# Activation sums by product, squares added by DMA, weight sums in place, and a down stage that begins with four units

## The chip, the cores and the metric

The kernel runs on one core of a Trainium2 chip. The metric is device time in microseconds for one execution of the whole program. A core has TensorE (matrix multiplication), VectorE, ScalarE, POOL (GpSimd) and SyncE, each with its own instruction order, and DMA queues that SyncE, ScalarE and POOL issue to.

## The reference

One decoder layer on 512 tokens of width 2048, in float32: a mixer of three head groups, a cross-attention into 256 memory tokens, and a gated MLP, each behind an RMSNorm and with a residual add; a last RMSNorm closes it. The change lies between the output projection of the cross-attention and the start of the MLP's down projection:

```python
def memory_cross_attention(h, mem_n, w_q, w_kv, w_o):
    ...
    return o @ w_o

def conv_ffn(h, w_up, conv_w, conv_b, w_down):
    S = h.shape[1]
    val, gate = jnp.split(h @ w_up, 2, axis=-1)
    gp = jnp.pad(gate, ((0, 0), (CONV_W - 1, 0), (0, 0)))
    g = conv_b
    for i in range(CONV_W):
        g = g + conv_w[i] * gp[:, i:i + S]
    return (jax.nn.silu(g) * val) @ w_down

    ...
    x = x + memory_cross_attention(rms_norm(x, norm_cross[l]), mem_n, w_cq[l], w_ckv[l], w_co[l])
    x = x + conv_ffn(rms_norm(x, norm_ffn[l]), w_up[l], conv_w[l], conv_b[l], w_down[l])
```

The MLP's inner width is 5504, that is 43 tiles of 128.

## The kernel before

Activations are kept transposed: 16 tiles (`x1`) of 128 channels by 512 tokens. Float32 accuracy comes from split operands: ScalarE copies a value to a rounded high half, VectorE subtracts it to get the low half, and a product is three multiplications (high-high, high-low, low-high; `mm3`, lines 352 to 354). Weights come from memory in raw tiles of 128 x 1024 (`wraw`, five buffers), which are split in two pieces of 512 columns into high and low halves (`whi`, `wlo`, five buffers each; `weights`, lines 338 and 339, and `split_weights`, lines 313 and 314).

**Output projection of the cross-attention** (`cross`, lines 1117 to 1130). Eight units; each loads one weight tile and computes two channel tiles with 24 multiplications on 512 columns. `resid` adds the result to `x1` on VectorE (line 959); `square` squares the new tile and adds it to one of two accumulators `sq`, in turn on VectorE and POOL (line 983; the first two squares are made on POOL, line 977). Then `token_sums` makes what the up stage needs of this unit.

**Up** (`up`, lines 1165 to 1238). The product of activations and up weights uses a scheme with seven products in place of eight: activations are cut in two by token halves (256) and by even and odd channel tiles, weights by value and gate columns and by even and odd channel tiles (raw tiles b11, b12, b22, b21). `token_sums` (line 1133) scales two channel tiles by the norm's gain (line 1139), makes four sums or differences of 256 columns on VectorE (line 1150), and splits seven operands (lines 1158 and 1159) into `sum` tiles or into slots of `xhi` and `xlo`. In `up`, `one(f)` does one of 43 units: four raw weight tiles, sums of them on VectorE (t1, t2, and in place b12; line 1192), seven calls of `product` with 24 multiplications on 256 columns each, results put together by VectorE and ScalarE, the norm factor R multiplied in, the causal conv and the gate (lines 1224 to 1229), and a store of the gated tile to memory (`gd`, line 1231). R is made in unit 0 from the two square accumulators (`rms`, line 434).

**Down** (`ffn`, lines 1240 to 1295). Two stages of five blocks of four gated tiles each; the last three tiles come in a closing part. In a stage the first two units (of eight; a unit is two channel tiles) go block by block as gated tiles are loaded back and split (`load`, lines 1249 to 1258), the other six then run over all five blocks. Results are scaled by R and added to `x1`.

PSUM has eight banks: four for the tag `acc`, four shared by all tags of `pst`. The planner that builds the program orders each engine's instructions by program order and by when it estimates their inputs and buffers to be ready, so an engine's order can differ from the text; within an engine and a queue the order is then fixed. Weights and gated tiles go through SyncE's queue. A pool opened where another was closed takes over its memory, each tile of it waiting for the tiles that lay there.

Of the kernel before, what the change touches and what calls it, by code (L numbers as in the profile page):

```python
# [48 lines left out]
SHIFT = 8  # L49
LEVELS = (64, 32, 16, 8, 4, 2, 1)  # L50
# [161 lines left out]
class _Trunk:  # L212
# [774 lines left out]
    def cross(self):  # L987
# [128 lines left out]
        self.sums = []  # L1116
        for u in range(8):
            w = self.weights(d["w_co"][u])
            pss = [self.acc(), self.acc()]
            for half in range(2):  # L1120
# [4 lines left out]
                self.resid(dt, pss[half], self.x1[dt], sqs, lambda n: wx.tile([P, n], F32, name="xsqt", tag="xsqt", bufs=2))  # L1125
            if u == 7:
                es_o.close()
                self.es_fa = ExitStack()
                sx = self.pool(self.es_fa, "fa", "left")
            self.sums.append(self.token_sums(u, sx, wx))  # L1130
        es_w.close()

    def token_sums(self, i, pool, tmp):
# [3 lines left out]
        for e in range(2):  # L1137
            t = tmp.tile([P, S], F32, name="y%d" % e, tag="y%d" % e, bufs=2)
            nc.scalar.activation(t, self.x1[2 * i + e], AF.Copy, scale=self.gain(2, 2 * i + e))
            y.append(t)  # L1140
        a11, a21 = y[0][:, :HT], y[0][:, HT:]
        a12, a22 = y[1][:, :HT], y[1][:, HT:]
        s = [tmp.tile([P, HT], F32, name="s%d" % n, tag="s%d" % n, bufs=2) for n in range(1, 5)]
        src = {1: a11, 6: s[1], 5: s[0], 7: s[2], 4: a22, 2: a12, 3: s[3]}
        made = {5: (a21, a22, ALU.add), 6: (s[0], a11, ALU.subtract), 7: (a11, a21, ALU.subtract),
                3: (a12, s[1], ALU.subtract)}
        out = {}
        for n, j in enumerate((1, 5, 6, 7, 4, 2, 3)):
            if j in made:
                nc.vector.tensor_tensor(src[j], made[j][0], made[j][1], op=made[j][2])  # L1150
            slot = 7 * i + n
            if slot < 2 * KT:
                tag = ("xhi", "xlo")[slot % 2]
                t, o = self.xp.tile([P, S], F32R, name=tag, tag=tag, bufs=KT), 0
            else:
                t, o = pool.tile([P, S + 16], F32R, name="sum%d" % slot), SHIFT
            th, tl = t[:, o:o + HT], t[:, o + HT:o + S]
            nc.scalar.activation(th, src[j], AF.Copy)  # L1158
            nc.vector.tensor_tensor(tl, src[j], th.bitcast(F32), op=ALU.subtract)  # L1159
            out[j] = (th, tl)  # L1160
        return out

    def up(self):
# [3 lines left out]
        fb = self.pool(es, "fb", "right")  # L1169
        gps = [fb.tile([P, S + 2], F32, name="gp%d" % i) for i in range(2)]  # L1170
# [7 lines left out]
        def raw(u):  # L1178
# [61 lines left out]
    def ffn(self):  # L1240
# [153 lines left out]
```

## Time and profile before

| what | value |
|---|---|
| median of 3 runs | 2396.06 us (2393.93 to 2398.09) |
| profiled execution, its own time | 2396.3 us |
| its span, first to last instruction | 2394.5 us |
| TensorE busy | 2342.9 us (98%) |
| VectorE busy | 1657.9 us (69%) |
| ScalarE busy | 1139.9 us (48%) |
| POOL busy | 87.6 us (4%) |
| mean granted clock of TensorE | 0.989 |

Times inside the profile count from the span's start. In the profile's rows PE is TensorE, PEld its weight loads, DVE VectorE, ACT ScalarE, SP or SPq SyncE's queue; L1158 is line 1158. A granted clock of 1.00 is 2.4 GHz, 0.50 is 1.2 GHz. A row of a timeline gives start, duration, engine, line, operation, output<-inputs and count. Operations on an engine overlap a little, so the distance between two starts is shorter than the duration.

### The profile page before, as it was taken

To read this page: it belongs to the slowest core of one execution; us is meant where nothing else is said; L and a number is where in the kernel's file an instruction comes from. 1 tells how busy PE (TensorE), PEld (TensorE's weight loads), DVE (VectorE), ACT (ScalarE), POOL (GpSimd) and SP (SyncE) were. 2 spreads that over 40 slices of the span, in tenths; PEclk is the share of its full clock that TensorE was granted. 3 is DMA by queue.
4 is the path that set the end of the run, shared out by engine and by line. 5 is a ranking of instruction groups with operands and counts; after the bars stand their busy time and mean duration, and the time that the engine had idled before them with its cause. 6 is when DMAs were issued, how large, how long until landed. Compare 5 with 4: busy or idle time off the path is not lost.

```text
span 2394.5 us, 37907 instructions
## 1 busy us (share of the span) xinstructions
PE 2342.9 (98%) x14514; PEld 2117.8 (88%) x14514; DVE 1657.9 (69%) x3112; ACT 1139.9 (48%) x2185; POOL 87.6 (4%) x91
## 2 busy tenths in 40 slices
PE   9999999999999999889999999999999899999997
PEld 8798898888878888689999999999999888888887
DVE  7725656667785375898888888888888743343336
ACT  6323346555664364655555555555555522232224
POOL 2000000000001000100000000000000000000003
PEclk9999999999999999989999999999999999999999
DMA  6432132322224352133333334333333533343332
GB/s 205 148 95 85 47 101 85 97 89 94 86 94 150 122 159 80 53 101 118 120 121 120 119 115 124 119 120 120 120 119 118 167 122 123 97 159 97 110 106 72
DMA packets 87458, 269.15 MB, mean 112 GB/s; under 512 B 9788, under 2 KB 14540, under 8 KB 87276
## 3 DMA queue, kind: packets, MB, share of 16 engines
q1 hardware_dynamic: 79504, 254.64, 33.1%
q10 hardware_dynamic: 7772, 12.09, 1.5%
q8 instruction: 114, 1.87, 0.3%
q14 instruction: 68, 0.56, 0.1%
HBM read 251.18 MB, written 19.45 MB: 113 GB/s over the span
## 4 chain that ended last, share of the span: by engine, by line
PE 93%; DVE 4%; ACT 1%; POOL 1%; DMA 0%; issue 0%; DVEq 0%; SPq 0%; POOLq 0%; ACTq 0%
PE acc L354 18%; PE acc L353 18%; PE acc L352 18%; PE psC L352 3%; PE psC L353 3%; PE psC L354 3%; PE acc L395 3%; PE acc L393 3%; PE acc L394 3%; PE psD L354 2%; PE psD L352 2%; PE psD L353 2%; PE psV L353 2%; PE psU L353 2%; PE psU L354 2%; PE psV L354 2%
## 5 line engine op out<-in xcount | busy, mean ns | idle before, releaser
L339 DVE TENSOR_TENSOR wlo<-wraw,whi 128x512 fp32r<-128x512 f32 (+2 forms) x496 | 336.6, 683 | 417.7 <-ACT whi L338 409.9
L338 ACT ACTIVATE whi<-wraw 128x512 fp32r<-128x512 f32 (+2 forms) x496 | 304.0, 617 | 631.6 <-PE acc L353 375.3
L352 PE MATMUL acc<-xhi,whi 128*128 128x512 f32 (+1 forms) x1518 | 550.8, 363 | 14.5 <-ACT xhi L1257 9.0
L354 PE MATMUL acc<-xhi,wlo 128*128 128x512 f32 (+1 forms) x1518 | 545.7, 360 | 0.0
L353 PE MATMUL acc<-xlo,whi 128*128 128x512 f32 (+1 forms) x1475 | 532.9, 361 | 0.0
L352 PEld LDWEIGHTS acc<-xhi,whi 128*128 128x128 f32 x1518 | 287.6, 190 | 53.7 <-ACT xhi L1257 9.2
L354 PEld LDWEIGHTS acc<-xhi,wlo 128*128 128x128 f32 x1518 | 287.7, 190 | 42.5 <-issue 0.8
L353 PEld LDWEIGHTS acc<-xlo,whi 128*128 128x128 f32 x1475 | 279.3, 189 | 39.5 <-issue 0.8
L313 ACT ACTIVATE whi<-wraw 128x512 fp32r<-128x512 f32 x344 | 215.2, 631 | 202.1 <-PE acc L353 71.0
L314 DVE TENSOR_TENSOR wlo<-wraw,whi 128x512 fp32r<-128x512 f32 x344 | 232.0, 685 | 32.9 <-ACT whi L313 32.4
L313 ACT ACTIVATE whi<-t 128x512 fp32r<-128x512 f32 x258 | 163.0, 633 | 158.7 <-PE acc L353 96.1
L314 DVE TENSOR_TENSOR wlo<-t,whi 128x512 fp32r<-128x512 f32 x258 | 173.3, 686 | 38.8 <-ACT whi L313 38.0
L352 PE MATMUL acc<-sum,whi 128*128 128x256 f32 x559 | 157.1, 281 | 2.2 <-ACT sum L1158 2.2
L353 PE MATMUL acc<-sum,whi 128*128 128x256 f32 x559 | 157.8, 282 | 0.5 <-DVE sum L1159 0.5
L354 PE MATMUL acc<-sum,wlo 128*128 128x256 f32 x559 | 157.3, 281 | 0.0
L353 PE MATMUL acc<-xhi,whi 128*128 128x256 f32 x430 | 121.6, 283 | 0.0
L393 PE MATMUL acc<-whi,xhi 128*128 128x384 f32 (+2 forms) x320 | 114.2, 357 | 1.5 <-ACT xhi L305 0.8
L395 PE MATMUL acc<-whi,xlo 128*128 128x384 f32 (+2 forms) x320 | 112.0, 351 | 0.4 <-DVE xlo L306 0.4
L394 PE MATMUL acc<-wlo,xhi 128*128 128x384 f32 (+2 forms) x320 | 112.2, 351 | 0.0
L354 PE MATMUL acc<-xlo,wlo 128*128 128x256 f32 x387 | 109.4, 283 | 0.0
L352 PE MATMUL acc<-xlo,whi 128*128 128x256 f32 x387 | 108.9, 281 | 0.0
L352 PEld LDWEIGHTS acc<-sum,whi 128*128 128x128 f32 x559 | 106.4, 190 | 2.4 <-ACT sum L1158 2.4
(369 smaller groups left out, 5246.1 us busy)
## 6 DMA issues: line engine op xcount, KB each, us to landing
wraw<-in_w_up SPq DMA_DIRECT2D x172, 512.0 KB, 3.7
wraw<-in_w_dn SPq DMA_DIRECT2D x80, 512.0 KB, 3.7
wraw<-in_w_o SPq DMA_DIRECT2D x32, 512.0 KB, 3.7
wraw<-in_w_qka SPq DMA_DIRECT2D x24, 512.0 KB, 3.7
gd<-cv SPq DMA_DIRECT2D x43, 256.0 KB, 4.3
graw<-gd SPq DMA_DIRECT2D x43, 256.0 KB, 4.1
wraw<-in_w_qkb SPq DMA_DIRECT2D x16, 512.0 KB, 3.6
xraw<-in_xT SPq DMA_DIRECT2D x15, 512.0 KB, 3.6
```

The costliest lines, as they stand in the source:

```text
L313: nc.scalar.activation(hi, r, AF.Copy)
L314: nc.vector.tensor_tensor(lo, r, hi.bitcast(F32), op=ALU.subtract)
L338: nc.scalar.activation(hi, r, AF.Copy)
L339: nc.vector.tensor_tensor(lo, r, hi.bitcast(F32), op=ALU.subtract)
L352: nc.tensor.matmul(out, lh, rh, start=start, stop=False, skip_group_check=more)
L353: nc.tensor.matmul(out, lh, rl, start=False, stop=False, skip_group_check=more)
L354: last = nc.tensor.matmul(out, ll, rh, start=False, stop=stop, skip_group_check=more)
L393: self.nc.tensor.matmul(o, xh[:, tt], wh, start=(k == 0), stop=False)
L394: self.nc.tensor.matmul(o, xh[:, tt], wl, start=False, stop=False)
L395: self.last = self.nc.tensor.matmul(o, xl[:, tt], wh, start=False, stop=(k == KT - 1))
```

## The change

- The activation sums are made for two units (four channel tiles) at a time, after every second unit of the output projection, with operations on 512 columns; the operands of one product lie together, and they are made in the order in which the products come, now 1, 5, 2, 6, 3, 4, 7. The sums' signs change with it.
- Weights of the output projection are requested two units ahead. During the last two units the first two up weight tiles are loaded, and the first and second products' weights are split there.
- Squares: all on ScalarE; the additions to the two accumulators become DMAs issued by POOL that add into their target.
- Up weight sums are made in place in b11 and b12; b22 has a pool of its own with two buffers, t1 and t2 are gone. A copy `s5` of product 5's result comes in, the value tile has two buffers.
- In the last up unit, four gated tiles are loaded into two raw weight buffers, ahead of product 7, and split after it in program order. In the first down stage the first four units, not two, go block by block; the other tiles of that stage are loaded by POOL's queue. The scratch for DMA descriptors doubles.

```diff
+NV = KT // 4
+UP_ORDER = (1, 5, 2, 6, 3, 4, 7)
...
+        slots = [(j, v) for j in UP_ORDER for v in range(NV)]
+        for j, v in slots[:KT]:
+            self.sums[j, v] = self.xslot() + (0,)
...
+        ws = [self.weights(d["w_co"][u]) for u in range(2)]
         for u in range(8):
-            w = self.weights(d["w_co"][u])
+            w = ws[u]
...
-                self.resid(dt, pss[half], self.x1[dt], sqs, lambda n: wx.tile([P, n], F32, name="xsqt", tag="xsqt", bufs=2))
-            if u == 7:
+                x1 = self.x1[dt]
+                nc.vector.tensor_tensor(x1, pss[half], x1, op=ALU.add)
+                if dt < 2:
+                    nc.scalar.activation(sqs[dt], x1, AF.Square)
+                else:
+                    sq = wx.tile([P, S], F32, name="xsqt", tag="xsqt", bufs=3)
+                    nc.scalar.activation(sq, x1, AF.Square)
+                    nc.gpsimd.dma_start(out=sqs[dt % 2], in_=sq, accum_op=ALU.add)
+            if u + 2 < 8:
+                ws.append(self.weights(d["w_co"][u + 2]))
+            elif u == 6:
+                first = [self.up_raw(i) for i in range(2)]
+                self.first = [first, self.halves(first[0])]
+            else:
+                nc.vector.tensor_tensor(first[0], first[0], first[1], op=ALU.add)
+                self.first.append(self.halves(first[0]))
...
-            self.sums.append(self.token_sums(u, sx, wx))
+            if u % 2:
+                self.token_sums(u // 2, wx)
...
+            t = tmp.tile([P, 2, S], F32, name="y%d" % e, tag="y%d" % e, bufs=2 - e)
+            for i in range(2):
+                k = 4 * v + 2 * i + e
+                nc.scalar.activation(t[:, i, :], self.x1[k], AF.Copy, scale=self.gain(2, k))
...
+        made = {5: (a22, a21, ALU.subtract), 6: (sa, a11, ALU.add), 3: (sb, a12, ALU.subtract),
+                7: (a21, a11, ALU.subtract)}
...
+            th, tl, o = self.sums[j, v]
+            th, tl = [t[:, o:o + S].rearrange("p (i c) -> p i c", c=HT) for t in (th, tl)]
             nc.scalar.activation(th, src[j], AF.Copy)
             nc.vector.tensor_tensor(tl, src[j], th.bitcast(F32), op=ALU.subtract)
...
+    def up_raw(self, u, pool=None):
+        if pool:
+            t = pool.tile([P, 1024], F32, name="b22", tag="b22", bufs=2)
+        else:
+            t = self.wp.tile([P, 1024], F32, name="wraw", tag="wraw", bufs=WR)
+        self.nc.sync.dma_start(out=t, in_=self.d["w_up"][u])
+        return t
...
+        b22s = [self.up_raw(2, fb)]
...
+            if f:
+                w1 = self.halves(b11)
+            product(1, w1, pa, True, True)
             nc.scalar.activation(s1, pa, AF.Copy)
...
-            tt(t1, b12, b11, ALU.subtract)
-            tt(t2, b22, t1, ALU.subtract)
...
+            if f:
+                tt(b11, b11, b12, ALU.add)
+                w5 = self.halves(b11)
+            product(5, w5, pc, True, True)
+            nc.scalar.activation(s5, pc, AF.Copy)
+            product(2, self.halves(b21), pa, False, True)
+            nc.scalar.activation(val[:, lo], pa, AF.Copy)
+            tt(b11, b11, b22, ALU.add)
+            product(6, self.halves(b11), pb, True, True)
+            tt(u2, s1, pb, ALU.subtract)
+            product(3, self.halves(b22), pc, False, True)
+            tt(b12, b12, b22, ALU.add)
+            tt(gp[:, 2:2 + HT], pc, u2, ALU.add)
...
+            tt(b11, b11, b21, ALU.add)
+            product(4, self.halves(b11), pd, True, True)
+            if f == FT - 1:
+                self.early = [self.wp.tile([P, 2, S], F32, name="wraw", tag="wraw", bufs=WR) for _ in range(2)]
+                for i, t in enumerate(self.early):
+                    for k in range(2):
+                        nc.sync.dma_start(out=t[:, k, :], in_=self.gd[2 * i + k])
+            product(7, self.halves(b12), pb, False, True)
+            if f == FT - 1:
+                for i in range(FB):
+                    src = self.early[i // 2][:, i % 2, :]
+                    self.gT[i] = self.xslot()
+                    nc.scalar.activation(self.gT[i][0], src, AF.Copy)
+                    nc.vector.tensor_tensor(self.gT[i][1], src, self.gT[i][0].bitcast(F32), op=ALU.subtract)
...
+            nc.vector.scalar_tensor_tensor(gp[:, 2:], gp[:, 2:], -1.0, self.R, op0=ALU.mult, op1=ALU.mult)
...
-            nc.sync.dma_start(out=raw, in_=self.gd[f])
+            (nc.gpsimd if f < FC[0][1] * FB else nc.sync).dma_start(out=raw, in_=self.gd[f])
...
+            if c0 == 0:
+                banks += [[self.acc(), self.acc()], [self.pst("U"), self.pst("V")]]
+            n = len(banks)
             for b in range(c0, c1):
                 need((b + 1) * FB)
-                for u in range(2):
+                for u in range(n):
                     part(b, u, banks[u], c0, c1)
-            for u in range(2):
-                add(u, banks[u])
-            for u in range(2, 8):
+                    if b == c1 - 1:
+                        add(u, banks[u])
+            for u in range(n, 8):
...
-    nc = bacc.Bacc("TRN2", target_bir_lowering=False, num_devices=1, dynamic_dma_scratch_size=1024)
+    nc = bacc.Bacc("TRN2", target_bir_lowering=False, num_devices=1, dynamic_dma_scratch_size=2048)
```

## Rows read from the trace of the kernel before

**Rows 1.** The page: busy time, and the chain that ended last, by engine

```profile
PE 2342.9 (98%) x14514; PEld 2117.8 (88%) x14514; DVE 1657.9 (69%) x3112; ACT 1139.9 (48%) x2185; POOL 87.6 (4%) x91
...
PE 93%; DVE 4%; ACT 1%; POOL 1%; DMA 0%; issue 0%; DVEq 0%; SPq 0%; POOLq 0%; ACTq 0%
```

**Rows 2.** Windows: stretch, length, busy by engine (instructions), clock, DMA share, GB/s

```profile
969.60:1024.00 54.40, 43.88 (x169) 33.67 (x168) 51.02 (x105) 38.62 (x87) 12.53 (x8) 0.91 0.18 59
1024.00:1057.50 33.50, 25.10 (x174) 23.92 (x172) 30.25 (x52) 18.95 (x36) 1.40 (x3) 0.80 0.23 74
1057.50:1895.20 837.70, 837.70 (x7058) 837.70 (x7056) 743.86 (x1132) 450.20 (x757) 0.00 (x0) 1.00 0.38 120
1895.20:1904.40 9.20, 0.22 (x2) 0.01 (x1) 3.98 (x7) 3.98 (x5) 0.00 (x0) 0.74 0.47 162
1904.40:1909.80 5.40, 5.38 (x12) 3.97 (x13) 4.61 (x7) 3.78 (x6) 0.00 (x0) 0.50 1.03 376
2200.00:2300.00 100.00, 100.00 (x443) 82.83 (x442) 38.56 (x59) 25.17 (x40) 0.00 (x0) 1.00 0.33 108
```

**Rows 3.** Waits of TensorE from 969.6 to 1057.5: total us, times, longest

```profile
PE acc L354 <- DVE wlo L339: 6.4, 4, 3.1
PE acc L352 <- ACT whi L313: 5.5, 1, 5.5
```

**Rows 4.** Waits of all engines from 1895 to 1910

```profile
PE acc L352 <- ACT xhi L1257: 9.0, 1, 9.0
```

**Rows 5.** Timeline of SyncE's queue from 1900.2 to 1913

```profile
1900.45 0.33 SPq L1231 DMA_DIRECT2D gd<-cv  x1
1900.83 11.96 SPq L1249 DMA_DIRECT2D graw<-gd  x16
```

**Rows 6.** Timeline of VectorE from 1034 to 1041

```profile
1035.21 1.22 DVE L1192 TENSOR_TENSOR wraw<-wraw 128x1024 f32<-128x1024 f32 x1
1036.34 2.49 DVE L314 TENSOR_TENSOR wlo<-t,whi 128x512 fp32r<-128x512 f32 x4
1038.75 0.68 DVE L445 TENSOR_TENSOR slo<-sq,shi 128x512 fp32r<-128x512 f32 x1
```

**Rows 7.** Timeline of VectorE from 999 to 1001.6

```profile
999.11 0.41 DVE L1150 TENSOR_TENSOR s<-s,y 128x256 f32<-128x256 f32 x1
999.45 0.41 DVE L1159 TENSOR_TENSOR xhi<-s,xhi 128x256 fp32r<-128x256 f32 x1
...
1000.19 1.45 DVE L1159 TENSOR_TENSOR xlo<-s,xlo 128x256 fp32r<-128x256 f32 x1
```

**Rows 8.** Timeline of ScalarE from 1002.9 to 1006.5

```profile
1002.97 0.61 ACT L981 ACTIVATE xsqt<-str 128x512 f32<-128x512 f32 x1
1003.50 0.71 ACT L1139 ACTIVATE y<-str,gains 128x512 f32<-128x512 f32 x1
1004.11 0.61 ACT L338 ACTIVATE whi<-wraw 128x512 fp32r<-128x512 f32 x1
```

**Rows 9.** Timeline of POOL from 999 to 1001.6

```profile
999.92 1.43 POOL L983 TENSOR_TENSOR sq<-sq,xsqt 128x512 f32<-128x512 f32 x1 [5.02 <-ACT xsqt L981]
```

**Rows 10.** Groups by line, 969.6 to 1040: busy us, mean ns, idle before

```profile
L983 POOL TENSOR_TENSOR sq<-sq,xsqt 128x512 f32<-128x512 f32 x7 | 11.3, 1615 | 43.5 <-ACT xsqt L981 43.5
...
L339 DVE TENSOR_TENSOR wlo<-wraw,whi 128x512 fp32r<-128x512 f32 x11 | 9.0, 828 | 0.0
...
L1159 DVE TENSOR_TENSOR xlo<-s,xlo 128x256 fp32r<-128x256 f32 x10 | 6.1, 616 | 0.0
L1150 DVE TENSOR_TENSOR s<-y 128x256 f32<-128x256 f32 x8 | 5.6, 704 | 0.5 <-ACT y L1139 0.4
```

**Rows 11.** DMA issues: tiles, queue, count, KB each, median us to landing

```profile
wraw<-in_w_up SPq DMA_DIRECT2D x172, 512.0 KB, 3.7
...
gd<-cv SPq DMA_DIRECT2D x43, 256.0 KB, 4.3
```

**Rows 12.** Waits of POOL from 950 to 1065

```profile
POOL gp L1172 <- ACT sum L1158: 2.0, 1, 2.0
```

More of the change, by code (lines that the diff above doesn't have):

```diff
@@ L1142, in token_sums @@
[L1142 to L1148, printed above, removed]
+        a11, a21 = y[0][:, :, :HT], y[0][:, :, HT:]
+        a12, a22 = y[1][:, :, :HT], y[1][:, :, HT:]
@@ L1149, in token_sums, with part @@
+        sa, sb = [tmp.tile([P, 2, HT], F32, name=n, tag=n, bufs=1) for n in ("sa", "sb")]
+        src = {1: a11, 2: a12, 4: a22, 5: sa, 6: sb, 3: sb, 7: sa}
+        made = {5: (a22, a21, ALU.subtract), 6: (sa, a11, ALU.add), 3: (sb, a12, ALU.subtract),
+                7: (a21, a11, ALU.subtract)}
+        def part(j):
             if j in made:
                 nc.vector.tensor_tensor(src[j], made[j][0], made[j][1], op=made[j][2])
[L1151 to L1156, printed above, removed]
@@ L1165, in up, with halves @@
+    def halves(self, w):
+        return [self.split_weights(w[:, h * 512:(h + 1) * 512]) for h in range(2)]
     def up(self):
@@ L1176, in cw, with product @@
             return self.conv[:, i * FT + f:i * FT + f + 1]
-        def raw(u):
-            t = self.wp.tile([P, 1024], F32, name="wraw", tag="wraw", bufs=WR)
-            nc.sync.dma_start(out=t, in_=d["w_up"][u])
-            return t
-        def product(j, w, ps, start, stop):
-            for h in range(2):
-                th, tl = self.split_weights(w[:, h * 512:(h + 1) * 512])
-                for k in range(4):
-                    i, c = 4 * h + k, slice(k * P, (k + 1) * P)
-                    self.mm3(ps, th[:, c], tl[:, c], *self.sums[i][j], start and i == 0, stop and i == NP - 1,
-                             more=True)
+        def product(j, parts, ps, start, stop):
+            for i in range(NP):
+                th, tl = parts[i // 4]
+                c = slice(i % 4 * P, (i % 4 + 1) * P)
+                sh, sl, o = self.sums[j, i // 2]
+                m = slice(o + i % 2 * HT, o + (i % 2 + 1) * HT)
+                self.mm3(ps, th[:, c], tl[:, c], sh[:, m], sl[:, m], start and i == 0, stop and i == NP - 1, more=True)
@@ L1191, in tt, with tmp @@
         def tt(out, a, b, op):
             nc.vector.tensor_tensor(out, a, b, op=op)
+        def tmp(name, n=HT, bufs=1):
+            return fb.tile([P, n], F32, name=name, tag=name, bufs=bufs)
         def one(f):
-            b11, b12, b22, b21 = [raw(4 * f + i) for i in range(4)]
+            if f == 0:
+                (b11, b12), w1, w5 = self.first
+                b22 = b22s[0]
+            else:
+                b11, b12 = self.up_raw(4 * f), self.up_raw(4 * f + 1)
+                b22 = self.up_raw(4 * f + 2, fb)
+            b21 = self.up_raw(4 * f + 3)
@@ L1196, in one @@
             pa, pb = self.acc()[:, :HT], self.acc()[:, :HT]
             pc, pd = self.pst("C")[:, :HT], self.pst("D")[:, :HT]
[L1198 to L1199 removed]
+            s1, s5, u2, u3 = tmp("s1"), tmp("s5"), tmp("u2"), tmp("u3")
+            val = tmp("val", S, 2)
             gp = gps[f % 2]
[L1201 removed]
+            if f:
+                w1 = self.halves(b11)
```

48 lines of the change are left out of this document (17 added, 31 removed).

## The prediction

> **What bounds the kernel now.** I read the page first, then busy time by stage, then the waits at the two places where TensorE stops, then single instructions. TensorE is busy for 98% of the span and stands in nearly every link of the chain that ended last [rows 1], so only what keeps TensorE from multiplying can be gained. By stage [rows 2]: the 42 up units after the first take 837.70 us with TensorE never idle, that is 7056 multiplications at 118.7 ns; the down stage runs 443 in 100 us, 225.7 ns each, also without a gap. No edit changes the number or width of these, so no gain lies there. Three stretches are left.
>
> First, units 1 to 7 of the cross-attention's output projection: 54.40 us for 168 multiplications worth 37.9 us, 16.5 us lost. Second, up unit 0: 33.50 us for 168 of 118.7 ns and four of 225.7 ns for the norm, worth 20.9 us, so 12.6 us lost. Third, the way from up to down: 9.20 us of standstill and then 5.40 us in which 12 multiplications worth 2.7 us ran, 11.9 us lost. Together 41.0 us: nothing in this change can gain more. The granted clock is 0.91 and 0.80 in the first two stretches and 0.50 right after the standstill [rows 2]: that is the 1.2 GHz level following each long stop, and part of what is lost.
>
> In the first two stretches VectorE is busy 51.02 of 54.40 us and 30.25 of 33.50 us, and TensorE waits for weight halves that ScalarE and VectorE have not split yet [rows 2, 3]. VectorE is the limit. In the third, TensorE waits 9.0 us for a split gated tile [rows 4]; the sixteen loads of gated tiles stand on SyncE's queue behind the store of the last gated tile, which comes out 5.3 us after the last up product [rows 5].
>
> **The change, part by part.**
>
> *Activation sums two at a time.* A VectorE operation on 512 columns costs 0.60 us in a row of four, a 1024-column one 1.13 us [rows 6]; on 256 columns 0.34 us from start to start [rows 7]. Before, one output unit has 11 sum operations of 0.34, two residual adds, two weight splits and one square add of 0.60: 6.7 us on VectorE against 5.4 us on TensorE. After, two units have 11 of 0.60, four adds and four splits: 11.4 us against 10.8 us, or 5.7 a unit. ScalarE has for two units four squares of 0.53, four scalings of 0.61 [rows 8], seven copies and four high halves, taken like a square at 0.53: 10.4 us. It is nearly full too, so some waits stay.
>
> *Squares added by DMA.* Beside a POOL add of 1.43 us [rows 9] a VectorE operation that otherwise takes 0.41 us takes 1.45 us [rows 7]; the seven POOL adds last 1.6 us each [rows 10]. The excess in three groups is 11 x (828 - 680) + 10 x (616 - 410) + 8 x (704 - 410) ns = 6.0 us [rows 10]. It goes, with the seven VectorE square adds (4.2 us). What comes: 14 DMAs of 256 KB issued by POOL, each of which must wait for the last on its accumulator, two chains of seven. No row shows such a DMA. The nearest are 256 KB to memory in 4.3 us and 512 KB from memory in 3.7 us [rows 11]; twice 4.3, for one that reads its target too, is the upper bound, half of 3.7, for half the bytes, the lower. I take 4.3: an output unit brings one link to each chain, so anything below 5.4 us stays hidden. Issuing them on POOL could hold VectorE as the adds did, 14 x 0.7 = 10 us, or not at all; I take nothing, since the collisions seen are beside instructions that read two tiles. The two clears of the conv tiles queue behind these DMAs on POOL; they are needed only late in unit 0. The two first squares move to ScalarE (1.1 us), in its slack.
>
> The Trainium skill (DMA: Bandwidth & Descriptors, "Anatomy of one DMA — SWDGE (gpsimd) path") gives such a DMA 2.0 us plus bytes over 436 GB/s, an estimate of 2.6 us here that no run here shows yet. By it the last square would be in 1.7 us earlier and the sum at most 1.7 us lower.
>
> *What is left of the first stretch.* Weights are now split two units ahead of the sums in VectorE's order, so a burst of sums (6.6 us) no longer stands between TensorE and its next weights. From the end of unit 1 VectorE has 12 adds, 11 splits, one in-place add and three bursts: 34.7 us, at the 94% it reached before [rows 2] 36.9 us, beside 32.5 us of TensorE. The 4.4 us too many are sums, for which TensorE does not wait yet. I leave 1.5 us of stalls: 54.4 becomes 39.4, **-15.0 us**. Ends: -16.5 (no stall), -7.
>
> *Up unit 0.* VectorE then owes the 4.4 us, the last burst of 6.6, the norm's five operations (3.0), ten splits (6.0), three in-place adds (3.4) and four small ones (1.3): 24.7 us, 26 us at 94%. The last half product follows, so unit 0 ends near 28 us instead of 33.5, **-5.5 us**. Ends: -12.6, and +4 if the order is bad. A new wait lies here: the third weight matrix goes to a pool that lies where the cross stage's temporaries lay. Before, the conv tiles' clear waited 2.0 us there for the sums [rows 12]; now the first buffer must wait for the last square's DMA: 0.6 + 0.5 + 4.3, load 3.7, in-place add 1.1, halves 1.2, so product 6 can start 11.4 us after the output projection instead of 8.6. VectorE's backlog covers that; without the backlog it costs 2.8 us. On SyncE's queue the loads for the second product and for unit 1 stand behind this load if they are ordered after it.
>
> *Weight sums in place.* The count on VectorE is the same (four of 1024 columns, 14 splits); a 256-column copy more on ScalarE, under 0.53 us a unit where it is 54% busy, and a norm multiply of another form lie beside TensorE [rows 2, 8]. VectorE has 837.70 - 743.86 = 93.8 us free over 42 units, 2.2 us each [rows 2]. New is a chain: product 5's weights wait for product 1's second half to be split, then 1.1 + 0.5 + 0.6 us. Five half buffers at 1.42 us of TensorE per half give four halves, 5.7 us, of lead; the chain leaves some 3 us. I cost it at nothing. Only three instead of four weight tiles per unit now share the five raw buffers, so the loads come no later. The second value buffer and the doubled DMA scratch cost no time.
>
> *Down.* Four gated tiles are loaded on SyncE before the last product and split there: 8 operations, 4 x 0.53 on ScalarE and 4 x 0.60 on VectorE in its slack. They take the buffers of the first product's sums, free 17 us earlier. Four units on the first four tiles give TensorE 4 x 24 x 225.7 ns = 21.7 us in which the other sixteen tiles, issued by POOL and so no longer behind the last store, have only to arrive. All eight banks are used; the first two pairs have been free for a unit. The down weights are loaded behind two fewer raw buffers: the first takes the tile of product 4, free some 8 us before the end, and lands after 3.7 us. I leave 0.9 us: 11.9 becomes 0.9, **-11.0 us**. Ends: -11.9, -4.
>
> **Sum.** -15.0 - 5.5 - 11.0 = -31.5 from the profiled execution's 2396.3 us (span 2394.5) gives 2364.8; the median of the runs lies 0.2 below that execution, so **2365 us**.
>
> **The rivals.**
> - *Every wait goes* (12%): no stall in unit 0 beyond the third weight's 2.8 us: 2396 - 16 - 10 - 12 = 2358.
> - *The backlog only moves* (20%): the sums saved in the first stretch come due in unit 0, which stays at 33.5, and ScalarE, nearly full, holds the first to -12: 2396 - 12 - 0 - 11 = 2373. For: VectorE has 35 us of work in 32. Against: 10 us of it are gone outright.
> - *Down finds a new wait* (8%): the second or third down weight stands behind the last gated store on SyncE's queue, as the tiles did [rows 5]; a stop of 4 us and as much at half clock return: 2372.
> - *The square chains set the pace* (5%): seven links of L us must fit beside units 1 to 7. At 8.6 us they take 60 us, ScalarE waits for one of three square buffers, weights with it: 2396 + 6 - 5 - 11 = 2386; slower from L = 10. The Trainium skill (DMA: Bandwidth & Descriptors, "Rules for kernel authors") also has an accumulating DMA wait for the semaphore of the one before it on the same bytes; no run here shows what goes wrong otherwise.
> - *Slower: the in-place chain stalls every unit* (6%). Place: between products 1 and 5, where VectorE also has the norm, conv and gate of the unit before, four operations of 0.60 and one of 0.34, 2.7 us; if that comes ahead of the in-place add, the 3 us of slack are gone. It decides from 31.5 / 42 = 0.75 us a unit; at 1.2 us it costs 50: 2415. Against: VectorE's order adapts, and the sums before came out in time with no wait at all.
> - *No change to be seen* (3%): the planner puts loads and sums back in the old places.
>
> **How the numbers follow.** The forecast itself has 46%, with 2358 to 2370 for its own range. The low end is all 41.0 us, 2355. The high end, 2383, takes half of the first stretch, nothing in unit 0 and 6 us in down; that leaves out the chain, the slow squares and little else, and the forecast's tail. A measurement tells 0.2%, 4.8 us, from no change. Faster: 46 + 12 + 20 + 8 and 3 of the 5 for the squares, 0.89; within 0.2%: 0.03; slower: 0.08.
>
> **What would show it.** Right: TensorE idle in the output projection below 3 us and no POOL add there; VectorE's longest sum near 0.7 us, not 1.4; unit 0 in 25 to 30 us; a down stage that starts within 1 us at full clock; up units still 19.9 us each. Wrong: a period over 20.2 us in up, idle behind an accumulating DMA, or a stop of several microseconds before product 2 or 6 or the first down unit.

## The result, and the profile after

The median falls from 2394.99 us (4 runs, 2393.92 to 2398.09) to 2368.69 us (4 runs, 2367.92 to 2370.96), ratio 0.989, 95% interval 0.9873 to 0.9907: 26.3 us less, where 31.5 were forecast. The profiled execution took 2368.75 us, its span 2367.0 us, 27.5 less than the span before.

Page of the changed kernel: busy time by engine, and DMA issues (KB each, median us to landing):

```profile
PE 2337.4 (99%) x14514; PEld 2116.1 (89%) x14514; DVE 1645.3 (70%) x3061; ACT 1137.4 (48%) x2202; POOL 95.0 (4%) x112
...
wraw<-in_w_up SPq DMA_DIRECT2D x129, 512.0 KB, 4.4
wraw<-in_w_dn SPq DMA_DIRECT2D x80, 512.0 KB, 3.7
...
gd<-cv SPq DMA_DIRECT2D x43, 256.0 KB, 2.1
```

The number of multiplications is the same [rows 1]; TensorE's share went from 98 to 99%. Windows of the changed kernel: units 1 to 7 of the output projection, up unit 0, up units 1 to 42, first of down; then unit 0 cut in three by the clock. The columns are those of [rows 2].

```profile
968.30:1006.40 38.10, 38.10 (x170) 31.55 (x169) 33.16 (x54) 32.49 (x58) 8.91 (x10) 1.00 0.66 151
1006.40:1037.40 31.00, 24.03 (x174) 22.66 (x173) 29.03 (x46) 21.01 (x38) 3.62 (x6) 0.89 0.52 136
1037.40:1879.90 842.50, 842.38 (x7058) 842.01 (x7057) 753.28 (x1140) 454.98 (x805) 1.69 (x3) 1.00 0.36 119
1879.90:1885.30 5.40, 5.40 (x26) 4.47 (x25) 4.35 (x9) 1.97 (x3) 2.16 (x4) 1.00 0.99 375
```

```profile
1006.40:1010.40 4.00, 2.05 (x17) 1.85 (x16) 4.00 (x8) 2.80 (x5) 1.74 (x2) 1.00 0.48 82
1010.40:1017.20 6.80, 4.29 (x18) 3.70 (x18) 6.09 (x10) 6.46 (x12) 1.88 (x4) 0.50 0.82 153
1017.20:1037.40 20.20, 17.69 (x143) 17.11 (x142) 18.94 (x30) 11.76 (x22) 0.00 (x0) 1.00 0.44 141
```

Beside [rows 2] that gives four terms. Units 1 to 7: 54.4 to 38.1, **-16.3**. Unit 0: 33.5 to 31.0, **-2.5**. Units 1 to 42: 837.7 to 842.5 for the same 7058 multiplications with TensorE never idle, **+4.8**: each now takes 119.3 instead of 118.7 ns. From up to down: 9.2 us of stop and 2.7 at half clock to nothing, **-11.9** (26 multiplications in 5.4 us at clock 1.00, where 12 went). These sum to -25.9; the first stretch also begins 1.3 us earlier (969.6 to 968.3), which makes -27.2 of the span's -27.5.

All stops of TensorE in the first two stretches, in the list of waits (total us, times, longest), and the three long ones in the timeline of TensorE (start, duration, in brackets the idle time before):

```profile
PE psC L354 <- ACT whi L315: 2.5, 1, 2.5
PE acc L356 <- DVE wlo L316: 2.3, 2, 1.9
PE acc L354 <- ACT s L1248: 2.1, 1, 2.1
```

```profile
1010.16 0.39 PE L356 MATMUL acc<-xhi,wlo 128*128 128x256 f32 x1 [1.95 <-DVE wlo L316]
...
1013.69 0.58 PE L354 MATMUL psC<-xhi,whi 128*128 128x256 f32 x1 [2.50 <-ACT whi L315]
...
1021.45 0.39 PE L354 MATMUL acc<-xhi,whi 128*128 128x256 f32 x1 [2.14 <-ACT s L1248]
```

All of them lie in unit 0, 6.9 us together; before, the two lines of [rows 3] had 11.9 us in five stops, and the whole list 18.9 us in eleven. A clock of 0.50, the 1.2 GHz level, follows the first stop, from 1010.4 to 1017.2. The first stop ends when VectorE has made the last low half of product 1's weights, which stands behind two low halves of sums in its order. The second, before product 5, waits for the first high half of the summed weights: the sum in place ends on VectorE at 1012.44, and ScalarE has one scaling between. The third is before product 2, which the prediction had named as a wrong sign: it adds into the bank that product 1 left, and the copy of that bank (line 1248) stands behind the last burst of sums in ScalarE's order. Timelines of VectorE and ScalarE at the first two stops, of ScalarE at the third, and of SyncE's queue:

```profile
1008.82 0.68 DVE L1186 TENSOR_TENSOR sl<-sb,sh 128x512 fp32r<-128x512 f32 x1
1009.42 0.68 DVE L316 TENSOR_TENSOR wlo<-wraw,whi 128x512 fp32r<-128x512 f32 x1
...
1011.23 1.21 DVE L1154 TENSOR_TENSOR wraw<-wraw 128x1024 f32<-128x1024 f32 x1
```

```profile
1013.02 1.13 ACT L315 ACTIVATE whi<-wraw 128x512 fp32r<-128x512 f32 x2
...
1018.69 0.63 ACT L1185 ACTIVATE sh<-sa 128x512 fp32r<-128x512 f32 x1 [0.57 <-DVE sa L1182]
1020.49 0.63 ACT L1185 ACTIVATE sh<-sb 128x512 fp32r<-128x512 f32 x1 [1.17 <-DVE sb L1182]
1021.03 0.36 ACT L1248 ACTIVATE s<-acc 128x256 f32<-128x256 f32 x1
```

```profile
1015.21 12.65 SPq L1198 DMA_DIRECT2D b<-in_w_up  x3
```

The third weight is issued at 1015.2, 8.8 us after the output projection. Its pool lies where the square buffers lay: it follows the last square's DMA but one, which landed at 1015.06; the very last, landed at 1016.57, let the next such load go. No multiplication waited for it. The groups of VectorE from 966 to 1040 that answer to [rows 10] (line, busy us, mean ns), and what reads or writes the square tiles (POOL's issues with their duration in ns, shortest, median, longest; who waited, us and times; to landing):

```profile
L316 DVE TENSOR_TENSOR wlo<-wraw,whi 128x512 fp32r<-128x512 f32 x15 | 9.9, 683 | 1.3 <-ACT whi L315 1.3
L341 DVE TENSOR_TENSOR wlo<-wraw,whi 128x512 fp32r<-128x512 f32 x11 | 7.2, 681 | 0.0
```

```profile
L1147 POOL DMA_DIRECT2D sq<-xsqt x14: 861/870/1071, 973.3 to 1013.2; - x14
...
  POOL sq L1147: 5.2, 2
  ACT xsqt L1146: 2.8, 2
...
DMA to landing us min/median/max: 3.3/4.0/7.3
```

The weight splits of 828 ns [rows 10] are back at 681 ns: no collision shows. The adding DMA took 4.0 us in the median, 4.3 were taken; the Trainium skill (DMA: Bandwidth & Descriptors, "Anatomy of one DMA — SWDGE (gpsimd) path") gave an estimate of 2.6 us, which lies under the shortest of the 14.

### The profile page after: what moved, and what is told of

The parts are those of the page before. It is cut to its first block, busy times and chain, and to the rows that moved or that the text cites. A ratio compares the mean times of both kernels' runs of the same rounds, so it can differ in the third digit from the quotient of the medians.

```text
span 2367.0 us, 38196 instructions
## 1 busy us (share of the span) xinstructions
PE 2337.4 (99%) x14514; PEld 2116.1 (89%) x14514; DVE 1645.3 (70%) x3061; ACT 1137.4 (48%) x2202; POOL 95.0 (4%) x112
## 3 DMA queue, kind: packets, MB, share of 16 engines
q1 hardware_dynamic: 77200, 250.45, 32.1%
## 4 chain that ended last, share of the span: by engine, by line
PE 94%; DVE 2%; ACT 1%; issue 1%; POOL 1%; DMA 1%; DVEq 0%; SPq 0%; POOLq 0%; ACTq 0%
PE acc L354 18%; PE acc L356 18%; PE acc L355 18%; PE psC L356 3%; PE psC L354 3%; PE psC L355 3%; PE acc L397 3%; PE acc L395 3%; PE acc L396 3%; PE psD L356 2%; PE psD L355 2%; PE psD L354 2%; PE psV L356 2%; PE psU L356 2%; PE psV L354 2%; PE psU L354 2%
## 5 line engine op out<-in xcount | busy, mean ns | idle before, releaser
L354 PE MATMUL acc<-xhi,whi 128*128 128x256 f32 (+1 forms) x2120 | 720.9, 340 | 2.1 <-ACT s L1248 2.1
L356 PE MATMUL acc<-xhi,wlo 128*128 128x256 f32 (+1 forms) x2120 | 715.7, 338 | 2.3 <-DVE wlo L316 2.3
L355 PE MATMUL acc<-xlo,whi 128*128 128x256 f32 (+1 forms) x2120 | 714.6, 337 | 0.0
L356 PEld LDWEIGHTS acc<-xhi,wlo 128*128 128x128 f32 x2120 | 402.8, 190 | 45.5 <-DVE wlo L316 2.9
L354 PEld LDWEIGHTS acc<-xhi,whi 128*128 128x128 f32 x2120 | 403.2, 190 | 40.7 <-ACT s L1248 2.3
L355 PEld LDWEIGHTS acc<-xlo,whi 128*128 128x128 f32 x2120 | 403.1, 190 | 39.0 <-issue 0.8
L316 DVE TENSOR_TENSOR wlo<-wraw,whi 128x512 fp32r<-128x512 f32 x516 | 346.7, 687 | 81.4 <-ACT whi L315 77.2
L1227 DVE TENSOR_TENSOR wraw<-wraw,b 128x1024 f32<-128x1024 f32 x86 | 104.8, 1219 | 1.4
L1227 DVE TENSOR_TENSOR wraw<-wraw 128x1024 f32<-128x1024 f32 x85 | 103.8, 1221 | 1.4
L354 PE MATMUL psC<-xhi,whi 128*128 128x256 f32 x344 | 98.1, 285 | 2.5 <-ACT whi L315 2.5
```

The costliest lines, as they stand in the source:

```text
L316: nc.vector.tensor_tensor(lo, r, hi.bitcast(F32), op=ALU.subtract)
L354: nc.tensor.matmul(out, lh, rh, start=start, stop=False, skip_group_check=more)
L355: nc.tensor.matmul(out, lh, rl, start=False, stop=False, skip_group_check=more)
L356: last = nc.tensor.matmul(out, ll, rh, start=False, stop=stop, skip_group_check=more)
L1227: nc.vector.tensor_tensor(out, a, b, op=op)
```

## The experiments

Each is the changed kernel with the edit shown, except e11. Times are of one execution, e12's apart; the kernel before beside them took 2392.59, 2395.12 and 2393.71 us. Stages that no edit touched began the first stretch between 967.4 and 971.5 us (e2 and e3 apart), so stretches are compared rather than totals.

### Why does an up unit take longer? (e1, e2, e3, e6, e9)

In the trace each of the 42 units is longer by 0.10 us, 20.05 instead of 19.95. Four things were new: the operands' addresses, their layout, the work beside, and the order in which operands come.

**e1**: sum tiles no longer shifted by 32 bytes.

```diff
-SHIFT = 8
+SHIFT = 0
```

> The changed kernel with one size altered: the twelve sum tiles outside the x slots start at the tile's first byte instead of 32 bytes in. In the changed kernel an up unit takes 20.05 us where it took 19.95 before, without TensorE ever idle: operands in x slots are multiplied in 120.0 ns, those in the shifted tiles in 118.4. Theory (place): what counts is where in a 64-byte line the moving operand begins; x slots begin at 0, the shifted tiles at 32. Then all 168 multiplications take 120.0 ns, an up unit 20.16 us, the whole some 4 to 5 us longer than the changed kernel. Rival (company): the pace comes from what else runs in up, the extra copy, sums in place, other loads; then a unit stays at 20.05 us and the total within 1 us.

2368.52 us; a unit takes 20.07 us, 0.02 more than with the shift, not 20.16. So where these tiles begin in a 64-byte line does not set their pace.

**e2**: a tile of 32 bytes ahead of the pool that holds the x slots (`xhi`, `xlo`), and the sum tiles that lie behind it moved on, so that they still begin 32 bytes into a 64-byte line.

```diff
+        nc.gpsimd.memset(self.xp.tile([P, 8], F32, name="xpad"), 0.0)
...
-                                            for n in ("sh", "sl")) + (SHIFT,)
+                                            for n in ("sh", "sl")) + (SHIFT + 8 * (v == NV - 1),)
```

> The changed kernel with 32 bytes put ahead of the x slots, so that these too begin 32 bytes into a 64-byte line (the sum tiles that lie behind them are moved on so that they stay at 32). Place: all 168 multiplications of a unit take 118.3 ns, a unit 19.88 us, 0.18 less than in the changed kernel and 0.07 less than in the kernel before; over 43 units 7 to 8 us, a total of 2361 us. Company: 20.05 us and 2369 us.

2374.8 us, but a unit falls to 19.73 us. **e3**: such a tile also ahead of the weights' pool, so that weights move by 32 bytes and x slots by 64.

> The changed kernel with the split weights moved to 32 bytes into a line while x slots stay at 0 and the other sum tiles at 32. It parts two forms of the place theory. If the moving operand's own place counts, nothing changes: x slots 120.0 ns, the others 118.4, a unit 20.05 us. If its place against the weights' counts, the two swap: x slots 118.3, the others 120.0, a unit 96 x 118.3 + 72 x 120.0 = 20.00 us. Company: 20.05 us with no change of either.

2377.98 us, a unit 19.71 us. Windows of units 1 to 42 of e2 and e3, and 100 us of down (512 columns) of e2:

```profile
1046.60:1876.00 829.40, 829.03 (x7058) 828.62 (x7057) 751.27 (x1140) 452.86 (x805) 1.69 (x3) 1.00 0.36 121
```

```profile
1048.00:1876.70 828.70, 828.31 (x7058) 827.90 (x7057) 750.43 (x1141) 452.77 (x805) 1.69 (x3) 1.00 0.36 121
```

```profile
2200.00:2300.00 100.00, 100.00 (x434) 80.97 (x433) 38.86 (x61) 25.52 (x41) 0.00 (x0) 1.00 0.32 104
```

Work, order and layout are those of the changed kernel, and 13 us are gone from up: the address decides. In e3 the slots begin at a multiple of 64 bytes again, and a unit is as short as in e2, so their place in a 64-byte line is not it. What e2 and e3 have in common is the distance of moving operand and weights, and I take that for what counts; that it is the slots' own address, over a longer stretch than 64 bytes, no run rules out. The swap that I expected of e3 did not come: its x slots take 116.7 ns, and the other sum tiles stay at 118.1. In the kernels before and after, an x slot lies a multiple of 512 bytes from its weights. The price stands in the last row: multiplications on 512 columns get slower by the same shift, 434 instead of 443 in 100 us (230 against 226 ns), so down and the early stages lose what up gains: the first stretch begins 9.2 us (e2) and 11.1 us (e3) later than in the changed kernel.

Distance alone does not tell before from after: x slots lay at a multiple of 512 bytes in both, with 32 of 56 operands. **e6** therefore puts the old layout back, with high and low half of one sum side by side in a slot and sums made unit by unit on 256 columns (the last two units' together):

```diff
-            if u % 2:
-                self.token_sums(u // 2, wx)
+            for w in ([u] if u < 6 else [6, 7] if u == 7 else []):
+                self.token_sums(w // 2, wx, w % 2)
...
-            th, tl = [t[:, o:o + S].rearrange("p (i c) -> p i c", c=HT) for t in (th, tl)]
+            if o:
+                th, tl = [t[:, o + i * HT:o + (i + 1) * HT] for t in (th, tl)]
+            else:
+                t = tl if i else th
+                th, tl = t[:, :HT], t[:, HT:]
```

> The changed kernel with the sums made unit by unit on 256 columns (the last two after the last unit, as their tiles are placed then) and with high and low half of an operand side by side in one x slot, as in the kernel before; product order, sums in place and all else stay. Theory (layout): where the halves lie makes the step from 19.95 to 20.05 us a unit; x-slot operands go from 120.0 to 119.0 ns and a unit to 19.95 us. Rival (order or company): the unit stays at 20.05 us. Beside it, sums on 256 columns cost VectorE 0.4 us and ScalarE 0.35 us more a unit: the 69.1 us of output projection and up unit 0 become 71 to 74 us; if the width of the sums does not matter there, they stay.

2370.65 us; a unit stays at 20.05 us, so layout and width are not it. What is left is the order. The timeline of TensorE inside up tells how it could matter (start, duration, operands): first the changed kernel, where the four products whose sums lie in x slots follow each other.

```profile
1299.78 0.28 PE L355 MATMUL acc<-xlo,whi 128*128 128x256 f32 x1
...
1301.46 0.28 PE L354 MATMUL psC<-xhi,whi 128*128 128x256 f32 x1
...
1302.90 0.28 PE L354 MATMUL psC<-xhi,whi 128*128 128x256 f32 x1
```

From the first row to the second are 14 multiplications and 1.68 us, from the second to the third 12 and 1.44 us: exactly 120 ns each. A unit has 96 of them in a row, then 72 on other sum tiles, at some 118.4 ns (20.05 less 96 x 0.120, over 72, is 118.5). In the kernel before every product took its first four or five units' sums from x slots, 12 or 15 multiplications, and the rest elsewhere.

**e9** goes back to that order alone:

```diff
-        slots = [(j, v) for j in UP_ORDER for v in range(NV)]
+        slots = [(j, v) for v in range(NV) for j in UP_ORDER]
```

> The sums that go into the x slots are chosen by unit pair (pairs 0 and 1 of all seven products and two of pair 2), as the kernel before had it, and not by product (products 1, 5, 2, 6 complete). Addresses and operations stay. Theory of runs: multiplications whose moving operand lies in an x slot settle at exactly 120.0 ns only after some seven of them in a row; before, such a row had 12 to 15 and the first seven took 116 to 119 ns, after the change it has 96. Then the period of an up unit falls from 20.05 to 19.95 us, 4 us over the stage, and the time comes to 2364 to 2368. Rival (the width of the sums or the new order of work on the other engines costs it): the period stays at 20.05. Down may start up to 1 us later, since the slots for the early gated tiles come free later.

2363.66 us. Windows of units 1 to 42, and the timeline of TensorE over one row of 18 multiplications on x slots:

```profile
1037.50:1874.60 837.10, 836.90 (x7059) 836.49 (x7058) 753.60 (x1140) 452.77 (x805) 3.85 (x7) 1.00 0.36 120
```

```profile
1299.95 0.27 PE L354 MATMUL psC<-xhi,whi 128*128 128x256 f32 x1
...
1300.65 0.28 PE L354 MATMUL psC<-xhi,whi 128*128 128x256 f32 x1
...
1302.09 0.28 PE L354 MATMUL psC<-sh,whi 128*128 128x256 f32 x1
```

A unit takes 19.91 us; the whole loss is gone, with a little more. The first six of the row took 0.70 us (117 ns each), the other twelve 1.44 (120 ns). Over all rows from 1070 to 1860 us the first six take 117.7 ns in the mean in e9 and 118.1 in the kernel before, the later ones 119.6 and 119.8; in the changed kernel not even the first six are quicker (120.6), and the other 90 take 120.0. So the order is what costs it: the change put 96 slow neighbours in a row, where shorter rows begin quicker. Why such a row settles at 120 ns stays open.

### The shift where it pays (e5, e11, e12)

**e5** makes the x slots (`xs`) one tile with 16 spare columns, and shifts by 32 bytes only the slots that hold sums, so that other stages keep their addresses:

```diff
+        self.xs, self.xn = self.xp.tile([P, 2 * KT * S + 16], F32R, name="xs"), 0
...
-    def xslot(self, n=S):
-        hi = self.xp.tile([P, n], F32R, name="xhi", tag="xhi", bufs=KT, padded_shape=[P, S])
-        lo = self.xp.tile([P, n], F32R, name="xlo", tag="xlo", bufs=KT, padded_shape=[P, S])
-        return hi, lo
+    def xslot(self, n=S, o=0):
+        a = self.xn % KT * S + o
+        self.xn += 1
+        return self.xs[:, a:a + n], self.xs[:, KT * S + a:KT * S + a + n]
...
-            self.sums[j, v] = self.xslot() + (0,)
+            self.sums[j, v] = self.xslot(S, SHIFT) + (0,)
```

> The changed kernel with the 32 x slots made one tile, so that a slot can be used 32 bytes in by the activation sums of up and unshifted by all other stages. The run with all x slots moved had up units of 19.72 us, 0.33 less than the changed kernel, but lost 9 us before up and 9 us in down, where multiplications are 512 columns wide. Theory (distance): 256-column products run faster, 512-column ones slower, when moving operand and weights lie 32 bytes apart modulo 512; then both are had here: up units 19.72 us, the stages before and behind as in the changed kernel, 13 to 15 us less, a total of 2354 to 2357 us. Rival: the slow stages were slow for another reason (all later buffers had moved too), and some of the 18 us stays: 2360 us or more.

2354.62 us. Windows of up unit 0 and units 1 to 42, and the timeline of TensorE (11 multiplications in 1.28 us, 116 ns each):

```profile
1007.60:1036.30 28.70, 23.28 (x174) 22.17 (x174) 26.70 (x42) 19.36 (x35) 3.41 (x6) 0.94 0.55 145
1036.30:1865.70 829.40, 829.02 (x7058) 828.60 (x7057) 751.25 (x1140) 452.98 (x805) 1.69 (x3) 1.00 0.36 120
```

```profile
1299.83 0.28 PE L357 MATMUL acc<-xs,wlo 128*128 128x256 f32 x1
...
1301.11 0.28 PE L356 MATMUL acc<-xs,whi 128*128 128x256 f32 x1
```

In down e5 has 443 multiplications in 100 us again, as in [rows 2], though its later buffers lie 64 bytes further on: the price of e2 hung on the slots' own shift.

**e11** is the kernel before with the same slots, and nothing of the change:

```diff
-                tag = ("xhi", "xlo")[slot % 2]
-                t, o = self.xp.tile([P, S], F32R, name=tag, tag=tag, bufs=KT), 0
+                if slot % 2 == 0:
+                    self.xcur = self.xslot(S, SHIFT)
+                t, o = self.xcur[slot % 2], 0
```

> The kernel before with nothing but the x slots of the activation sums shifted by 32 bytes. If the distance of moving operand and weights sets the pace whatever the change, an up unit falls from 19.95 to 19.73 us, 43 units give 9 us, and the time comes to 2383 to 2387 beside a kernel before of 2392 to 2396; the change is then worth about 30 us on either footing. If the shift helps only the order of the changed kernel: 19.9 us or more a unit and 2391 to 2396.

2385.33 us, a unit 19.74 us; its units 1 to 42 in the windows:

```profile
1054.90:1884.00 829.10, 828.98 (x7056) 828.78 (x7054) 738.50 (x1132) 444.49 (x758) 0.00 (x0) 1.00 0.39 121
```

Shifted, both kernels run up at the same pace, and the change is worth 2385.33 - 2354.62 = 30.7 us, near the forecast's 31.5. That is one execution of each; taken each from the kernel before beside it, it is 40.5 - 8.4 = 32.1 us. **e12** is e5 again, timed five times:

> The kernel of e5 once more (the x slots of the activation sums shifted by 32 bytes in up alone), now timed in rounds against the kernel before. If the single look was typical: median 2353 to 2357 and a ratio of 0.983 to 0.985 to the kernel before. If the look was a lucky draw of the earlier stages, which lay within 3 us of each other in the other looks: 2357 to 2360.

Median 2356.00 us (5 runs, 2355.15 to 2358.14), ratio to the kernel before 0.9833, interval 0.982 to 0.9847. Its interval lies wholly under the changed kernel's (0.9873 to 0.9907): it beats the kernels before and after.

### What made the first two stretches shorter? (e4, e6, e10)

**e4** puts the squares' additions back on VectorE and POOL, and the first two squares on POOL:

```diff
-                if dt < 2:
-                    nc.scalar.activation(sqs[dt], x1, AF.Square)
-                else:
-                    sq = wx.tile([P, S], F32, name="xsqt", tag="xsqt", bufs=3)
-                    nc.scalar.activation(sq, x1, AF.Square)
-                    nc.gpsimd.dma_start(out=sqs[dt % 2], in_=sq, accum_op=ALU.add)
+                self.square(dt, x1, sqs, lambda n: wx.tile([P, n], F32, name="xsqt", tag="xsqt", bufs=3))
```

> The changed kernel with the squares added as before, in turn by POOL and VectorE, no adding DMA. In the changed kernel units 1 to 7 of the output projection and up unit 0 take 69.1 us together (38.1 and 31.0). Theory (collisions): VectorE gets 4.2 us of adds and some 6 us of collisions back; as it is the limit there, the 69.1 us become 76 to 79 us and single sums of 1.2 us or more show beside POOL adds. Rival (slack): ScalarE's waits for the square DMAs (2.8 us in the changed kernel) go, which makes up for it, and the stretch stays at 68 to 71 us.

2378.64 us. Windows of the two stretches, a group of VectorE from 966 to 1050, and one collision in the timelines of VectorE and POOL:

```profile
970.10:1013.60 43.50, 38.80 (x169) 31.21 (x169) 41.47 (x61) 32.21 (x57) 9.82 (x7) 1.00 0.23 73
1013.60:1047.10 33.50, 26.91 (x173) 25.63 (x174) 30.64 (x46) 20.71 (x37) 3.70 (x4) 0.85 0.28 93
```

```profile
L341 DVE TENSOR_TENSOR wlo<-wraw,whi 128x512 fp32r<-128x512 f32 x11 | 11.0, 1032 | 0.0
```

```profile
1001.79 1.19 DVE L341 TENSOR_TENSOR wlo<-wraw,whi 128x512 fp32r<-128x512 f32 x1
```

```profile
1000.87 1.56 POOL L985 TENSOR_TENSOR sq<-sq,xsqt 128x512 f32<-128x512 f32 x1 [8.58 <-ACT xsqt L983]
```

77.0 us for both stretches against 69.1: the DMAs are worth 7.9 us, 5.4 of them in the output projection. The splits go from 681 to 1032 ns in the mean, since some run beside a POOL addition, as the one above, which takes 1.19 us. By the Trainium skill (SBUF — State Buffer, "Who interferes with whom") a VectorE instruction with two inputs in SBUF contends with a GpSimd instruction that reads SBUF; such a subtraction holds only the shared read interface, while descriptor generation is taken to need the write interface. Both agree here: 1032 ns in the mean where POOL adds, 681 where it issues 14 DMAs; the split at 1009.42, shown above, took 0.68 us with an issue beside it from 1009.32 to 1010.19.

**e6** (above) tells what the width of the sums is worth:

```profile
969.10:1007.20 38.10, 38.10 (x169) 31.53 (x168) 37.61 (x92) 35.47 (x82) 9.27 (x11) 1.00 0.71 153
1007.20:1038.80 31.60, 24.13 (x173) 22.58 (x172) 27.00 (x51) 20.25 (x42) 3.24 (x6) 0.95 0.51 131
```

With 256-column sums VectorE is busy 37.61 of 38.10 us, and TensorE still never stops there: 69.7 us for both against 69.1. The width gives 0.6 us, no more than these two stretches differ without any edit in them (68.4 and 68.5 us in e7 and e8, below). Of the 87.9 us before, e4's 77.0 leave 10.9 us for the rest of the change in these stretches; the width takes 0.6 of that. Some 10 are left, by subtraction, to the other parts together: weights requested and split ahead of the sums, the first up weights loaded early, the sums in a new order. I take the first of these for the main one, since TensorE waited for weight halves [rows 3]; no run undid any of them alone.

**e10** is e5 with five square buffers, paid for with one buffer fewer for the first scaled tile:

```diff
-                    sq = wx.tile([P, S], F32, name="xsqt", tag="xsqt", bufs=3)
+                    sq = wx.tile([P, S], F32, name="xsqt", tag="xsqt", bufs=5)
...
-            t = tmp.tile([P, 2, S], F32, name="y%d" % e, tag="y%d" % e, bufs=2 - e)
+            t = tmp.tile([P, 2, S], F32, name="y%d" % e, tag="y%d" % e, bufs=1)
```

> The x slots shifted by 32 bytes in up alone, as in the run of that edit, and five buffers in place of three for the squares that the DMAs read, paid for with one buffer in place of two for the first scaled tile. Theory: ScalarE waited 1.8 to 2.8 us for a square buffer behind the adding DMAs; without that the splits and sums are done earlier and up unit 0 falls from 28.6 by 1 to 2 us, time 2352 to 2354. Rival: the single buffer of the scaled tile holds ScalarE instead, or unit 0 hangs on VectorE's backlog and the late copy of product 1's result: 2354 to 2358, unit 0 not under 28.5.

2354.53 us. ScalarE no longer waits for an adding DMA, but unit 0 is 28.3 us (28.7 in e5) and its two long stops are those of e5 (2.7 and 2.2 us there):

```profile
PE psC L355 <- ACT whi L316: 2.4, 1, 2.4
PE acc L355 <- ACT s L1249: 2.2, 1, 2.2
```

So the time of the DMAs is not what unit 0 still loses. Whether an earlier copy of product 1's result (line 1248) would take the second stop away was not tried.

### Which part of the new beginning of down does the work? (e7, e8)

**e7** lets two units, not four, go block by block; **e8** loads no gated tile ahead of product 7 (both `if f == FT - 1` parts of `one` out, so that all twenty tiles come as the other sixteen do).

```diff
-            if c0 == 0:
+            if c0 < 0:
                 banks += [[self.acc(), self.acc()], [self.pst("U"), self.pst("V")]]
```

> The changed kernel with two units instead of four going block by block in the first down stage; early tiles and POOL loads stay. Theory (early tiles alone): the first tiles end the stop, and 10.9 us on two units are enough for the next four tiles, which POOL's queue brings: TensorE idle at the start of down under 1 us, total within 1 us of the changed kernel. Rival (four units needed): the next tiles come too late, a stop of 3 to 6 us before the second block, total up by 3 to 9 us.

> The changed kernel without the early load of the first four gated tiles: they are loaded by POOL's queue like the other sixteen; four units first stay. Theory (early tiles needed): the tiles' buffers lie where up's temporaries lay, so the loads start after the last products, and TensorE stands for 4 to 8 us and then runs at half clock for some microseconds: total up by 5 to 10 us. Rival (the store in front was all): off SyncE's queue the tiles come in time, idle under 1.5 us, total within 2 us.

2372.65 and 2379.96 us. Waits of TensorE around the beginning of down, e7 and then e8, and two windows of e8:

```profile
PE acc L354 <- ACT xhi L1315: 1.1, 1, 1.1
```

```profile
PE acc L354 <- ACT xhi L1304: 7.5, 1, 7.5
```

```profile
1880.40:1888.10 7.70, 0.17 (x3) 0.01 (x1) 4.62 (x10) 4.04 (x6) 2.16 (x4) 0.85 0.87 319
1888.10:1893.00 4.90, 4.90 (x12) 3.64 (x13) 4.28 (x7) 3.06 (x6) 3.59 (x7) 0.54 0.58 200
```

Without early tiles the stop is 7.5 us and the clock falls to its lower level after it, as in [rows 2]: 12 multiplications of 226 ns in 4.9 us lose 2.2 more, so that some 10 of the 11.9 us come back. With two units the early tiles still close all but 1.1 us, at full clock. The total of e7 is 3.9 us above the changed kernel's; 3.2 of them are there before its first stretch begins (971.5 against 968.3), as is 1.0 of e8's 11.2. The four tiles carry this part; the four units add about 1 us.

## Why the prediction was right, and where its terms were off

- **Units 1 to 7 (-15.0, measured -16.3).** Right in size, but one of its reasons falls. I counted on fewer, wider sums to get VectorE under TensorE; e6 does without and loses nothing there, with VectorE at 99% busy. So its load by itself was not the limit. Two reasons that I had named beside it are left: the collisions, which e4 shows (5.4 us here), and that weights are split ahead of the sums, which is argued by subtraction alone.
- **Squares by DMA (4.3 us each, hidden).** Right: 4.0 in the median, and no stop of TensorE is put down to one. ScalarE waited 2.8 us for them (1.8 in e5, where taking that away gave 0.3 us in the two stretches: e10). The bounds 1.9 and 8.6 held every one of them (3.3 to 7.3). That their issue does not hold VectorE, taken at nothing, is right too (681 ns a split); the 0.7 us an issue of the other end stands in no row, and POOL took 0.87.
- **Up unit 0 (-5.5, measured -2.5).** The step that put the end at VectorE's 26 us failed: unit 0 took 31.0, beyond the 25 to 30 of the sign. TensorE does not stop after 1025.2, 12 us before the unit's end, so it was not the sum of VectorE's work that set the end, but what came late at the beginning: product 1's last low half behind sums on VectorE (1.95 us), product 5's first high half behind the sum in place (2.5), the copy of product 1's bank behind the last sums on ScalarE (2.1). The half clock after the first stop had no term either: 18 multiplications in 4.29 us of busy time, 2.1 us more than at 119 ns. The third weight's wait was there, and covered by the backlog, as written, but it was issued 8.8 us into the unit where my terms gave 5.4, and behind the last square's DMA but one.
- **Weight sums in place (0; right), but "up units still 19.9 us each" (measured 20.05).** The chain between products 1 and 5 never stalled TensorE, so the slower side's rival of 2415 us is out. What failed is the sentence that no edit changes the width of multiplications, so none changes their price: the list of which sums lie in x slots was costed at nothing and cost 4.8 us. e9 took it back.
- **Down (-11.0, measured -11.9).** Right, by the early tiles (e8: 10 us) more than by the four units (e7: 1.1 us). The other sixteen came in time by POOL's queue: TensorE has no wait from 1878 to 1930. Whether SyncE's queue would have done as well, no run shows.
- **Sum.** The earlier stages gave 1.3 us that no term had. -16.3 - 2.5 + 4.8 - 11.9 - 1.3 = -27.2 for -31.5. That the total is only some 4 us off is in part luck: two terms fell short by 7.8 us (unit 0 by 3.0, up by 4.8), and 3.5 us more than forecast elsewhere, 1.3 of them from stages that the change does not touch, made up for some of it. The backlog rival (2373) was partly true: over half of unit 0's gain did move away, but the first stretch was not held back.

## What to carry to other kernels

Where an engine is never idle its time can still change: compare the spacing of single instructions between two traces before an order or an address is costed at nothing. Ask of a change that makes an engine's work cheaper whether the engine was late by its load or by its order; here wide sums gave 0.6 us and an end of the collisions 7.9, and some 10 are left to the order of the work (by subtraction). A handful of operands made ready early, enough to cover the load behind them, is worth more than a longer runway for all of them.

## What the runs showed of the hardware

- TensorE's pace on 256 columns changed with the address of the moving operand: 120 ns at a distance from the weights of a multiple of 512 bytes in long rows (some 118 over the first six of the short rows of e9 and of the kernel before), and 117 ns at 32 bytes more. On 512 columns it is the other way round: 226 ns at a multiple of 512 bytes, 230 at 32 more (e2; 232 in e3, 431 in 100 us). The Trainium skill (SBUF — State Buffer, "Who interferes with whom") gives TensorE independent read ports for the moving operand and for weights; by these runs the pace still changes by 3% with the distance of the two, or with the slots' own address, which no run parts from it. Why was not found.
- The store of a gated tile lands in 2.1 us in the median after the change and took 4.3 before [rows 11], while an up weight's load went from 3.7 to 4.4 and a down weight's stayed at 3.7. No run asked why.
